# A hybrid attention block on one core: two weight loads taken out of line, earlier

## Chip, cores and metric

The kernel runs on 1 of the cores of a Trainium2 chip, as one program. The metric is the device time of one execution in microseconds (us); where several executions were timed, their median.

## What is computed

One decoder block over 512 tokens of width 2048, all float32: a norm of x, one wide projection, two groups of eight (A) and sixteen (B) heads, a gate, an out-projection with the residual, and a last norm.

```python
h = _rmsnorm(x, norm_g[l])
proj = h @ w_in[l]
(qa, kca, vca, ksa, vsa, kwa, vwa, za, ga, qb, kb, vb, zb) = jnp.split(proj, offsets, axis=-1)
...
y_a = o_a.reshape(B, S, WIDTH_A) * jax.nn.silu(za)    # compressed, selected and window attention, gated
qb = _rope(_heads(qb, N_HEADS_B, HEAD_DIM_B)).reshape(B, S, N_KV_B, GROUP_B, HEAD_DIM_B)
o_b = _banded_attention(qb, _rope(_heads(kb, N_KV_B, HEAD_DIM_B)), _heads(vb, N_KV_B, HEAD_DIM_B),
                        WIN_B, sink=sinks[l].reshape(N_KV_B, GROUP_B))
y_b = o_b.reshape(B, S, WIDTH_B) * jax.nn.silu(zb)
x = x + jnp.concatenate([y_a, y_b], axis=-1) @ w_out[l]
return _rmsnorm(x, final_g)
```

The second group is B. Its keys come from 128 columns of `w_in`, which the kernel calls `wkb` and loads as two units of 128 x 1024.

## The kernel before

**Split words.** TensorE (PE) multiplies in a reduced float32 format. Every operand is therefore split into a high word, made by a copy on ScalarE (ACT), and a low word, the rest, made by a subtraction on VectorE (DVE); a product is three matmuls (`mm3`, lines 119 to 121): high by high, high by low, low by high. A weight unit of 128 x 1024 is loaded by `load_unit` (L85): SyncE (SP) queues the DMA into a raw buffer (L88), ACT makes `whi` (L92), DVE makes `wlo` (L93).

**Buffers.** There are four raw buffers of one tile each, raw0 to raw3. `raw()` (L78) hands out raw0, raw1, raw2 in turn; raw3 lies in another pool and is used by the pairs of group A only, and later, in group B, by every second query tile `qs`. The split words have three buffers. A load into a raw buffer waits until its last reader is done, and a split waits until the matmuls on its word buffer are done.

**Group A.** For heads 1 to 7, `pair(h)` (L662) makes a head's query and gate projections together from four quarter units x1 to x4 of `wq`, each in one of the four raw buffers, by sums of the units (L672) and seven products on halves of x. For head 7 x1 lies in raw3, x2 in raw2, x4 in raw1 and x3 in raw0. The sums are x2+=x4, x4+=x1, x2+=x1 and x2+=x3, in this order; x1 is last read by x2+=x1, x4 by its split, x3 by x2+=x3 and x2 by the last split. `attn_a(h)` is the head's attention: scores `sp` (L546), exponentials `tt` on ACT (L562), scaling (L574), transposes `tp` (L584), the split words `ph` (ACT, L514) and `pl` (DVE, L515) of the transposed weights, and the products `op` (L590 to L607). While the pairs run, half of the even tiles of `xh` and `xl` hold other data.

**Between the groups.** `swap_x` (L626) loads the halves of `xh` and `xl` back from `xd`, as four DMAs (L630). Then `proj(wkb, parity=1)` (L882) starts group B: both wkb units are loaded first, the odd tiles of x are multiplied first, then the even ones. `proj(wz[16])` (L883) is the first query projection.

**Group B and the out-projection.** For i from 0 to 7: softmax of head pair i, the query projection of i + 1 from `wz[17 + i]`, the gate projection from `wz[24 + i]`, and `attn_b(i)`, which ends in two copies of `op` into `ob` on ACT (L877). Afterwards y is split (`yh`, L915) into memory that x held, and multiplied by the eight units of `wo0` (L1010).

**Order.** The program text is not the order of execution. A scheduler orders each engine's instructions by its own estimates, and each engine then runs its list in order, waiting on semaphores; so does SP with its DMAs. `tc.issue_after(a)` adds an instruction's wait for `a`. In group A and B, instructions of several heads and projections interleave on every engine.

Of the kernel before, what the change touches and what calls it, by code (L numbers as in the profile page):

```python
# [10 lines left out]
F32 = mybir.dt.float32  # L11
F32R = mybir.dt.float32r
AF = mybir.ActivationFunctionType
# [4 lines left out]
P = 128  # L18
# [10 lines left out]
MOVING, EVEN, STILL = 0, 16, 32  # L29
# [6 lines left out]
def hybrid_block(ctx, tc, xT, xtm, w0, w1s, w2s, wz, wq, wkb, wo0, wos, cw1, cw2, cpos, rope, tabs, sinks, gT, fg, out):  # L36
    nc = tc.nc
    pe, act, dve, pool = nc.tensor, nc.scalar, nc.vector, nc.gpsimd
# [32 lines left out]
    last = {}  # L71

    raws = [0]

    def weights(tag):
        return (wk if tag == "raw3" else wp).tile([P, 1024], F32, name="raw", tag=tag, bufs=1)

    def raw():  # L78
        raws[0] += 1
        return weights(f"raw{raws[0] % 3}")  # L80

    def words(place):
        return [wp.tile([P, 1088], F32R, name=nm, tag=nm)[:, place:place + 1024] for nm in ("whi", "wlo")]

    def load_unit(src, width, rawp=None, opening=False, place=EVEN):  # L85
        rw = rawp.tile([P, 1024], F32, name="raw", tag="raw") if rawp else raw()
        hi, lo = words(place)
        last["dma"] = (nc.scalar if opening else nc.sync).dma_start(rw[:, :width], src).ins  # L88
        if opening:
            dve.tensor_copy(hi[:, :width], rw[:, :width])  # L90
        else:
            last["hi"] = act.activation(hi[:, :width], rw[:, :width], AF.Copy).ins  # L92
        last["lo"] = dve.tensor_tensor(out=lo[:, :width], in0=rw[:, :width], in1=hi[:, :width].bitcast(F32),  # L93
                                       op=ALU.subtract).ins
        return hi, lo
# [77 lines left out]
    for k in range(KT):  # L173
        if k == 0:
            hi, lo = load_unit(w0[0, :, 0, 0:512], 512, opening=True)
            xr = load_x(k)
        else:
            xr = load_x(k)
            hi, lo = load_unit(w0[0, :, k // 2, (k % 2) * 512:(k % 2) * 512 + 512], 512)
# [88 lines left out]
    even = [x.rearrange("p (m e) s -> p e m s", e=2)[:, 0, :, 0:256].bitcast(F32) for x in (xh, xl)]  # L268
# [54 lines left out]
    for u in range(KT // 2):  # L323
        hi, lo = load_unit(w0[1, :, u], 1024)
# [58 lines left out]
    for g in range(2):  # L383
        act.activation(KH[g][:, 0:CMP], kct[:, g * 32:g * 32 + 32], AF.Copy)
        dve.tensor_tensor(out=KL[g][:, 0:CMP], in0=kct[:, g * 32:g * 32 + 32], in1=KH[g][:, 0:CMP].bitcast(F32),
                          op=ALU.subtract)
# [6 lines left out]
    for u in range(8):  # L393
# [6 lines left out]
            writes.pop(0)()  # L400
        if u in (2, 3, 5, 6):
            build()
    def proj(src, parity=None, jobs=None):
        ps = psp.tile([P, S], F32, name="pj", tag="pj")
        ready = []
        ks = list(range(KT))
        if parity is not None:
            ks = list(range(parity, KT, 2)) + list(range(1 - parity, KT, 2))
        for i, k in enumerate(ks):
            while len(ready) < (2 if jobs or parity is not None or k >= 8 else 1):  # L410
                ready.append(load_unit(src[:, len(ready)], 1024))
            if jobs and i in jobs:
                jobs[i]()
            hi, lo = ready[k // 8]
            js = slice((k % 8) * P, (k % 8) * P + P)
            mm3(ps, hi[:, js], lo[:, js], xh[:, k, :], xl[:, k, :], i == 0, i == KT - 1)
        return ps
# [42 lines left out]
    def z_evac(ps):  # L460
        zr = wk.tile([P, S], F32, name="zr", tag="t2", bufs=1)
        st = wk.tile([P, S], F32, name="st", tag="st")
        dve.tensor_tensor(out=zr, in0=ps, in1=rstdb, op=ALU.mult)
        act.activation(st, zr, AF.Tanh, scale=0.5)
        dve.scalar_tensor_tensor(out=st, in0=st, scalar=1.0, in1=zr, op0=ALU.add, op1=ALU.mult)
        return st

    def q_rope(ps, cos, sin, t1=None):
        if t1 is None:
            t1 = wk.tile([P, S], F32, name="t1", tag="t1", bufs=1)  # L470
        t2 = wk.tile([P, S], F32, name="t2", tag="t2", bufs=1)
        rope_mul(t1, t2, ps, cos, sin)
        pool.tensor_tensor(out=t1, in0=t1, in1=t2, op=ALU.add)
        return t1
# [151 lines left out]
    def swap_x(source):  # L626
        for part in range(2):
            ms = slice(4 * part, 4 * part + 4)
            for e in range(2):
                nc.sync.dma_start(even[e][:, ms], source[e, :, ms])  # L630

    def forms_back(f, ms):
        for e, (v, k) in enumerate(((VH, KH), (VL, KL))):
# [90 lines left out]
    for h in range(8):  # L724
        if h < FIRST:
            qq = q_evac(q0, cosA, sinA)
            st = z_evac(proj(wz[8], 0))
            lows, highs = slice(0, 4), slice(4, 8)
            first = []
            with tc.issue_after(last["dma"]):  # L730
                first.append(load_quarter(wq[0], tags[0], 3))
                forms_back(0, lows)
                forms_back(1, lows)
            for c, quarter in zip(tags[1:], (0, 2, 1)):
                with tc.issue_after(last["dma"]):
                    first.append(load_quarter(wq[0], c, quarter))
            with tc.issue_after(last["dma"]):
                for f in (2, 3):
                    forms_back(f, lows)
                    forms_back(f, highs)  # L740
        else:
            qq, st = pair(h, *first) if h == FIRST else pair(h)
        attn_a(h, *qq, st)
        if h == 3:
            for e in range(2):
                nc.sync.dma_start((KH, KL)[e][0].bitcast(F32), Kd[e])
            for e in range(2):
                nc.sync.dma_start((VH, VL)[e][:, 0].rearrange("p t w c -> p (t w c)").bitcast(F32), Vd[e])
# [10 lines left out]
    cosB, sinB = cosA, sinA  # L759
# [90 lines left out]
    def attn_b(i, tts, st):  # L850
        g = i // 4
        op = psob.tile([P, 2, S], F32, name="opb", tag="opb")
        for kt in (0, 2, 3, 1):
            tp = pst.tile([P, S], F32, name="tp", tag="tp")
            nsl = 2 if kt < 3 else 1
            for v in range(2):
                for s in range(nsl):
                    qt = kt + s
                    c0 = 0 if (s == 1 or qt == 0) else P
                    o = (v * nsl + s) * P  # L860
                    pe.transpose(tp[:, o:o + P], tts[qt][:, v, c0:c0 + P], ident)  # L861
            oc = op[:, :, kt * P:(kt + nsl) * P]
            if nsl == 2:
                ph, pl = split_pt(tp)
                for v in range(2):
                    es = slice(v * 256, v * 256 + 256)
                    pe.matmul(oc[:, v], VB[:, kt, g, :], ph[:, es], start=kt == 0, stop=False)
                    pe.matmul(oc[:, v], VB[:, kt, g, :], pl[:, es], start=False, stop=kt == 1)
            else:
                pd = wk.tile([P, 256], F32, name="pd", tag="pd", bufs=1)  # L870
                act.activation(pd, tp[:, 0:256], AF.Copy)
                for v in range(2):
                    pe.matmul(oc[0:64, v], vbf[:, kt, g * 64:g * 64 + 64], pd[:, v * P:v * P + P], start=False, stop=False)
        ob = wb.tile([P, S], F32, name="ob", tag="ob")
        for v in range(2):
            hs = slice(v * 64, v * 64 + 64)
            act.activation(ob[hs], op[64:128, v, :], AF.Copy)  # L877
            dve.tensor_tensor(out=ob[hs], in0=op[0:64, v, :], in1=ob[hs], op=ALU.add)
        finish(8 + i, ob, st)

    kb1 = wk.tile([P, S], F32, name="kb1", tag="xr", bufs=1)
    q_rope(proj(wkb, parity=1), cosB, sinB, kb1)  # L882
    q2 = qb_evac(proj(wz[16]), 0)  # L883
    build_k(kb1, 0)
    build_v()
    for i in range(8):
        tts = softmax_b(i, q2)
        if i < 7:
            q2 = qb_evac(proj(wz[17 + i]), i + 1)
        if i == 0:  # L890
            build_k(kb1, 1)
        st = z_evac(proj(wz[24 + i]))
        if i == 7:
            psb.close()
            xstack.close()
            so1 = ctx.enter_context(sb("so1", side="right"))
            yh = [so1.tile([P, S], F32R, name=f"yh{f}") for f in range(16)]
            yl = [so1.tile([P, S], F32R, name=f"yl{f}") for f in range(16)]
            psf1 = ctx.enter_context(tc.tile_pool(name="psf1", bufs=2, space=PSUM, side="right"))
        attn_b(i, tts, st)  # L900
        if i in (1, 2, 3, 4):
            y_back(i - 1)
# [105 lines left out]

    acc = banks(0)
    for u in range(8):  # L1010
        hi, lo = load_unit(wo0[:, u], 1024)
        for j in range(2):
            f = 2 * u + j
            ws = slice(j * 512, j * 512 + 512)
            for t in range(NQ):
                ts = slice(t * P, (t + 1) * P)
                mm3(acc[t], yh[f][:, ts], yl[f][:, ts], hi[:, ws], lo[:, ws], f == 0, f == 15)
        combos(u)
# [3 lines left out]
    for t in range(NQ):  # L1022
        v = xs0[t // 2][:, t % 2, :]
# [18 lines left out]
    for n in range(1, 4):  # L1042
        xs.append([late(2 * n - 2 + T) for T in range(2)])
        src = wos[n - 1]
# [287 lines left out]
```

## Time and profile before

| | us |
|---|---|
| median of 3 runs | 826.01 |
| the three runs | 823.29, 826.01, 827.65 |
| the profiled execution | 823.73 |
| its span, first to last instruction | 822.0 |
| outside the span | 1.73 |
| PE busy | 805.1 |
| DVE busy | 664.5 |
| ACT busy | 484.0 |

The profile is one execution; its times are us from the start of the span. "Busy" leaves out waiting, branching and issuing of DMAs. Matmuls are pipelined, so the duration of one is longer than its distance from the next, and the starts tell how fast PE goes. An idle time in brackets stands before the instruction, with what ended it. "SPq" is the queue in which SP issues DMAs; the time beside it is that of the issue, not of the transfer.

### The profile page before, as it was taken

How to read it: one execution, taken by the hardware profiler on the slowest of the kernel's cores; microseconds unless marked ns; L12 is line 12 of the kernel's file. 1: busy time of each engine (PE TensorE's matmuls, PEld its weight loads, DVE VectorE, ACT ScalarE, POOL GpSimd, SP SyncE). 2: the span in 40 equal slices, each digit the busy share in tenths (PEclk: the TensorE clock that was granted, in tenths of full speed). 3: DMA queues.
4: the chain of work that ended last, by engine and by line, in shares of the span. 5: the costliest groups of instructions: out<-in, count | busy, mean ns of one | idle time of the engine just before them, and what ended most of it. 6: DMA issues, size and time to landing. Idle time of an engine off the chain costs nothing.

```text
span 822.0 us, 14132 instructions
## 1 busy us (share of the span) xinstructions
PE 805.1 (98%) x5278; PEld 731.4 (89%) x5278; DVE 664.5 (81%) x1326; ACT 484.0 (59%) x1026; POOL 67.1 (8%) x54
## 2 busy tenths in 40 slices
PE   9999999999999999999999999999999999999996
PEld 7788898989999999999888888888888888999996
DVE  6869786967889899899766688887687798877895
ACT  6744456564767687786665365645444657543545
POOL 3600002020000000000011121011001000110000
PEclk9999999999999999999999999999999999999998
DMA  9665886899321332423633321222222227797845
GB/s 326 197 205 167 279 289 208 262 332 331 103 89 29 116 84 91 163 91 112 227 111 102 99 90 57 77 80 76 77 78 77 78 61 253 226 264 188 252 90 205
DMA packets 52116, 128.30 MB, mean 156 GB/s; under 512 B 4944, under 2 KB 17232, under 8 KB 52048
## 3 DMA queue, kind: packets, MB, share of 16 engines
q1 hardware_dynamic: 50032, 120.59, 44.4%
q0 software_dynamic: 1728, 6.29, 4.4%
q8 instruction: 41, 0.67, 0.3%
q10 hardware_dynamic: 288, 0.52, 0.2%
q14 instruction: 27, 0.22, 0.1%
HBM read 110.31 MB, written 17.07 MB: 155 GB/s over the span
## 4 chain that ended last, share of the span: by engine, by line
PE 78%; DVE 8%; DMA 7%; ACT 4%; issue 3%; SPq 0%; DVEq 0%; ACTq 0%; POOLq 0%
PE pj L121 14%; PE pj L120 14%; PE pj L119 14%; PE bank L121 4%; PE bank L119 4%; PE bank L120 4%; PE oa L120 3%; PE oa L121 3%; PE oa L119 3%; PE sp L546 3%; DMA rw<-wos 2%; PE tp L861 2%; DVE wlo L624 1%; PE tp L584 1%; DMA xr<-xT 1%
## 5 line engine op out<-in xcount | busy, mean ns | idle before, releaser
L121 PE MATMUL pj<-xh,wlo 128*128 128x512 f32 (+1 forms) x560 | 194.7, 348 | 1.8 <-DVE wlo L624 1.8
L119 PE MATMUL pj<-xh,whi 128*128 128x512 f32 (+1 forms) x560 | 195.0, 348 | 1.4 <-ACT whi L92 1.4
L120 PE MATMUL pj<-xl,whi 128*128 128x512 f32 (+1 forms) x560 | 194.6, 347 | 0.0
L93 DVE TENSOR_TENSOR wlo<-raw,whi 128x1024 fp32r<-128x1024 f32 (+2 forms) x102 | 115.4, 1134 | 35.2 <-ACT whi L92 34.3
L92 ACT ACTIVATE whi<-raw 128x1024 fp32r<-128x1024 f32 (+1 forms) x101 | 95.1, 944 | 75.1 <-PE pj L120 21.5
L121 PEld LDWEIGHTS pj<-xh,wlo 128*128 128x128 f32 x560 | 105.4, 188 | 15.3 <-DVE wlo L624 2.4
L119 PEld LDWEIGHTS pj<-xh,whi 128*128 128x128 f32 x560 | 105.3, 188 | 13.9 <-ACT whi L92 1.6
L120 PEld LDWEIGHTS pj<-xl,whi 128*128 128x128 f32 x560 | 105.3, 188 | 12.8 <-issue 0.7
L624 DVE TENSOR_TENSOR wlo<-raw,whi 128x1024 fp32r<-128x1024 f32 x49 | 59.5, 1221 | 9.3 <-ACT whi L623 9.2
L623 ACT ACTIVATE whi<-raw 128x1024 fp32r<-128x1024 f32 x49 | 51.1, 1054 | 21.7 <-PE pj L120 6.2
L120 PE MATMUL oa<-wlo,yh 128*128 128x256 f32 (+1 forms) x168 | 50.2, 299 | 0.4 <-DVE wlo L1160 0.4
L119 PE MATMUL oa<-whi,yh 128*128 128x256 f32 (+1 forms) x168 | 49.9, 298 | 0.6 <-ACT yh L915 0.6
L121 PE MATMUL oa<-whi,yl 128*128 128x256 f32 (+1 forms) x168 | 49.5, 298 | 0.0
L840 ACT ACTIVATE ttb<-ttb,sums 128x256 f32<-128x256 f32 (+1 forms) x64 | 30.1, 471 | 26.3 <-DVE sums L833 25.8
L514 ACT ACTIVATE ph<-tp 128x512 fp32r<-128x512 f32 x56 | 32.3, 592 | 22.3 <-PE tp L584 16.2
L515 DVE TENSOR_TENSOR pl<-tp,ph 128x512 fp32r<-128x512 f32 x56 | 38.0, 686 | 4.5 <-ACT ph L514 4.3
L120 PE MATMUL bank<-wlo,xh 128*128 128x256 f32 (+1 forms) x128 | 40.1, 316 | 0.1
L121 PE MATMUL bank<-whi,xl 128*128 128x256 f32 (+1 forms) x128 | 39.7, 312 | 0.0
L119 PE MATMUL bank<-xh,whi 128*128 128x512 f32 x96 | 36.8, 394 | 1.3 <-ACT whi L92 1.0
L119 PE MATMUL bank<-whi,xh 128*128 128x256 f32 (+1 forms) x128 | 36.5, 317 | 1.3 <-ACT whi L92 1.3
L120 PE MATMUL bank<-xl,whi 128*128 128x512 f32 x96 | 36.9, 390 | 0.0
L562 ACT ACTIVATE tt<-tt,sums 128x128 f32<-128x128 f32 (+3 forms) x64 | 35.3, 554 | 1.6 <-DVE sums L552 1.5
(356 smaller groups left out, 2169.3 us busy)
## 6 DMA issues: line engine op xcount, KB each, us to landing
raw<-wz SPq DMA_DIRECT2D x36, 512.0 KB, 3.9
raw<-wq SPq DMA_DIRECT2D x28, 512.0 KB, 4.0
raw<-cw SPq DMA_DIRECT2D x16, 512.0 KB, 5.1
raw<-wos SPq DMA_DIRECT2D x12, 512.0 KB, 5.4
rw<-wos SPq DMA_DIRECT2D x10, 512.0 KB, 4.8
xr<-xT SPq DMA_DIRECT2D x16, 256.0 KB, 4.8
raw<-w SPq DMA_DIRECT2D x8, 512.0 KB, 4.2
fd<-ft SPq DMA_DIRECT2D x4, 1024.0 KB, 6.0
```

What stands on the lines that cost most here:

```text
L92: last["hi"] = act.activation(hi[:, :width], rw[:, :width], AF.Copy).ins
L93: last["lo"] = dve.tensor_tensor(out=lo[:, :width], in0=rw[:, :width], in1=hi[:, :width].bitcast(F32), op=ALU.subtract).ins
L119: pe.matmul(ps, ah, bh, start=first, stop=False, skip_group_check=go_on)
L120: pe.matmul(ps, ah, bl, start=False, stop=False, skip_group_check=go_on)
L121: recent["mm"] = pe.matmul(ps, al, bh, start=False, stop=last, skip_group_check=go_on).ins
L514: act.activation(ph, tp, AF.Copy)
L515: dve.tensor_tensor(out=pl, in0=tp, in1=ph.bitcast(F32), op=ALU.subtract)
L546: pe.matmul(sp[:, a:b], qq[:, qs], kk[0][:, ko:ko + b - a], start=pi == 0, stop=pi == 2)
L562: act.activation(tv, tv, AF.Exp, bias=mn[:, i, 1 + w:2 + w], scale=-1.0, accum_out=dn[:, i, 1 + w:2 + w])
L623: act.activation(hi, src, AF.Copy)
L624: last["lo"] = dve.tensor_tensor(out=lo, in0=src, in1=hi.bitcast(F32), op=ALU.subtract).ins
L840: act.activation(tv, tv, AF.Exp, bias=mn[:, e, v:v + 1], scale=-1.0, accum_out=dn[:, e, v:v + 1])
```

## The change

Three things. While head 7's pair is written down, the two units of `wkb` get the buffers raw3 and raw1, and their DMAs are tied behind the pair's last load, the second behind the first. `swap_x`'s four DMAs are tied behind the last weight load, so behind both. `proj(wkb)` takes the loaded buffers; `raws[0] += 1` makes the rotation of raw0 to raw2 skip one place, so every later unit lies one buffer further than before (the first unit of `wz[16]` in raw1, where it lay in raw2). Second, the first unit of `wo0` is loaded and split after the gate projection of i = 6, ahead of that of i = 7, whose two units so come after it. Third, head pair 6's two copies into `ob` wait for that unit's ACT split. In the built order of each engine, lists are the same up to head 7, differ in places through the start of group B, and are nearly the same from there on.

```diff
-    def load_unit(src, width, rawp=None, opening=False, place=EVEN):
-        rw = rawp.tile([P, 1024], F32, name="raw", tag="raw") if rawp else raw()
+    def load_unit(src, width, rawp=None, opening=False, place=EVEN, loaded=None):
+        if loaded is None:
+            rw = rawp.tile([P, 1024], F32, name="raw", tag="raw") if rawp else raw()
+            last["dma"] = (nc.scalar if opening else nc.sync).dma_start(rw[:, :width], src).ins
+        else:
+            rw = loaded
         hi, lo = words(place)
-        last["dma"] = (nc.scalar if opening else nc.sync).dma_start(rw[:, :width], src).ins
...
-    def proj(src, parity=None, jobs=None):
+    def proj(src, parity=None, jobs=None, loaded=()):
...
-                ready.append(load_unit(src[:, len(ready)], 1024))
+                ready.append(load_unit(src[:, len(ready)], 1024,
+                                       loaded=loaded[len(ready)] if loaded else None))
...
     def swap_x(source):
...
-                nc.sync.dma_start(even[e][:, ms], source[e, :, ms])
+                with tc.issue_after(last["dma"]):
+                    nc.sync.dma_start(even[e][:, ms], source[e, :, ms])
...
             qq, st = pair(h, *first) if h == FIRST else pair(h)
+        if h == 7:
+            early = []
+            for u in range(2):
+                early.append(weights(("raw3", "raw1")[u]))
+                with tc.issue_after(last["dma"]):
+                    last["dma"] = nc.sync.dma_start(early[u], wkb[:, u]).ins
         attn_a(h, *qq, st)
...
-            act.activation(ob[hs], op[64:128, v, :], AF.Copy)
+            with ExitStack() as behind:
+                if i == 6:
+                    behind.enter_context(tc.issue_after(last["hi"]))
+                act.activation(ob[hs], op[64:128, v, :], AF.Copy)
...
-    q_rope(proj(wkb, parity=1), cosB, sinB, kb1)
+    raws[0] += 1
+    q_rope(proj(wkb, parity=1, loaded=early), cosB, sinB, kb1)
...
         st = z_evac(proj(wz[24 + i]))
+        if i == 6:
+            first_out = load_unit(wo0[:, 0], 1024)
...
-        hi, lo = load_unit(wo0[:, u], 1024)
+        hi, lo = load_unit(wo0[:, u], 1024) if u else first_out
```

## Prediction

> **What bounds the kernel now.** I read the page first, then the PE's waits, then windows of 60 us, and only then the stretch in which the change works. The page's engine rows and its chain:
>
> ```profile
> span 822.0 us, 14132 instructions
> ...
> PE 805.1 (98%) x5278; PEld 731.4 (89%) x5278; DVE 664.5 (81%) x1326; ACT 484.0 (59%) x1026; POOL 67.1 (8%) x54
> ...
> PE 78%; DVE 8%; DMA 7%; ACT 4%; issue 3%; SPq 0%; DVEq 0%; ACTq 0%; POOLq 0%
> ```
>
> TensorE (PE) is busy for 805.1 of 822.0 us: all that any reordering can win is in the 17 us left, and most of those are in the opening and the end. Where the change works, the windows (us; busy time of PE, PEld, DVE, ACT, POOL; granted clock; DMA share; GB/s) say:
>
> ```profile
> 400.00:405.00 5.00, 3.09 (x22) 2.46 (x22) 2.26 (x5) 2.66 (x6) 0.00 (x0) 1.00 1.05 376
> ...
> 420.00:480.00 60.00, 60.00 (x320) 51.45 (x319) 37.79 (x77) 31.14 (x65) 10.64 (x6) 1.00 0.32 103
> 480.00:540.00 60.00, 60.00 (x331) 51.28 (x330) 51.72 (x156) 36.05 (x102) 4.50 (x2) 1.00 0.22 71
> ```
>
> One hole of 1.91 us at 400 to 405, with the DMA engines full (share 1.05), and then no idle PE at all. The page "Perfetto Trace Analysis" of the Trainium skill, section Identifying the Most-Contended Engine, would judge PE's headroom by the weight loads' busy share, not by the matmuls'. By that rule 89% on the page leaves 11%, some 90 us. The rows differ: where PE waits for nothing (420 to 540) PEld stands at 51.4 of 60, so about 86% is full here, and I take nothing from that headroom.
>
> **The hole that the first edit is to close.** The PE timeline (start, duration, operation, idle before it and what ended that), and the chain of waits over the same stretch:
>
> ```profile
> 401.61 0.28 PE L120 MATMUL pj<-pu,whi 128*128 128x256 f32 x1
> 401.73 0.28 PE L121 MATMUL pj<-pu,wlo 128*128 128x256 f32 x1
> 403.45 0.50 PE L119 MATMUL pj<-xh,whi 128*128 128x512 f32 x1 [1.45 <-ACT whi L92]
> 403.79 0.40 PE L120 MATMUL pj<-xl,whi 128*128 128x512 f32 x1
> 404.64 0.39 PE L590 MATMUL op<-ph,VH 128*128 128x256 f32 x1 [0.46 <-ACT ph L514]
> 404.86 0.39 PE L121 MATMUL pj<-xh,wlo 128*128 128x512 f32 x1
> 405.09 0.39 PE L119 MATMUL pj<-xh,whi 128*128 128x512 f32 x1
> ```
> ```profile
> 395.44 6.82 DMA raw<-wkb
> ```
>
> Matmuls overlap, so I cost a stall by starts: a 256-column one takes 0.12 us (401.61 to 401.73), a 512-column one 0.23 (404.86 to 405.09). From 401.73 to 403.45 is 1.72, so 1.60 lost; from 403.79 to 404.64 is 0.85, so 0.62 lost. Together **2.22 us**. Both come from one transfer, the wkb unit that is issued at 395.44 and lands at 402.26. ScalarE (ACT) shows how one late load makes two stalls:
>
> ```profile
> 396.04 1.06 ACT L623 ACTIVATE whi<-raw 128x1024 fp32r<-128x1024 f32 x1
> ...
> 402.34 1.06 ACT L92 ACTIVATE whi<-raw 128x1024 fp32r<-128x1024 f32 x1 [2.41 <-DMA raw<-wkb]
> 403.30 0.71 ACT L562 ACTIVATE tt<-tt,sums 128x512 f32<-128x512 f32 x1
> ...
> 404.01 0.57 ACT L514 ACTIVATE ph<-tp 128x512 fp32r<-128x512 f32 x1
> ```
>
> ACT stands at L92 for 2.41 us, and behind it wait an exponential (L562) and the copy ph (L514) for which PE waits next. The DMA queue of SyncE (SP) tells why the load is late:
>
> ```profile
> 387.99 0.33 SPq L88 DMA_DIRECT2D raw<-wkb  x1
> 394.43 0.37 SPq L630 DMA_DIRECT2D xl<-xd  x1
> 394.89 0.46 SPq L630 DMA_DIRECT2D xh<-xd  x1
> 395.44 0.45 SPq L88 DMA_DIRECT2D raw<-wkb  x1
> ...
> 398.38 0.34 SPq L88 DMA_DIRECT2D raw<-wz  x1
> 400.95 0.33 SPq L496 DMA_DIRECT2D yd<-st  x1
> ...
> 407.53 0.39 SPq L501 DMA_DIRECT2D yp<-yd  x1
> ```
>
> By the built order the load at 387.99 is the second wkb unit (buffer raw1). The first takes raw0, which the last sum of pair(7) frees, and stands behind two loads of x's halves.
>
> **Edit 1, part by part.** Removed: the place at 395.44. Added: nothing; the same two transfers and splits. Moved: the first unit goes to raw3, whose last reader is the sum x2+=x1, and the second stays in raw1 but is queued second:
>
> ```profile
> 389.07 1.22 DVE L672 TENSOR_TENSOR raw<-raw 128x1024 f32<-128x1024 f32 x1
> ```
>
> That ends at 390.29, so both are queued by 390.8, ahead of x's halves. A load of this size takes
>
> ```profile
> L88 SPq DMA_DIRECT2D raw<-wkb x2: 333/394/454, 388.0 to 395.4; - x2
> ...
> DMA to landing us min/median/max: 3.6/5.2/6.8
> ```
>
> 3.6 us (the one issued at 388, alone) to 6.8 (among the halves): the first lands between 393.9 and 397.1, and I take 394, the row without company. Even 397.1 does: in the built order the split L92 now stands right after L623, whose row ends at 397.10. It then ends at 398.2, PE asks for it at 401.85, and its DVE half (1.13 us, a row below) has until two matmuls later. ACT had been free since 399.93 (402.34 less 2.41), so the exponential (0.71) and ph (0.57) then end at 401.2, while PE's new order has twelve 512-column matmuls (2.7 us) ahead of ph's product: needed at 404.6. Both stalls go: minus 2.22 us, and 0 at the other end if something else takes their place.
>
> Moved past on SP: x's halves start 0 to 1 us later, for the tail of the second wkb load. In place of the late wkb unit a wz unit (the z projection's, into raw0) is now queued among them, so they land about when they do now. PE's order has pair(7)'s last product and half of wkb's own matmuls ahead of them, and no wait of PE's in this trace names them. Cost 0; without that cover 1 us. The first unit of wz[16], issued now at 398.38 into raw2, goes into raw1 instead, behind the second wkb split and behind yp<-yd: about 408. It is the one thing that becomes late, and the rival below prices it. Later units come three buffers ahead as before; between 420 and 540 PE waits for nothing, and the rest of the schedule, being PE-bound, moves up whole.
>
> **Edit 2.** The out-projection's first unit is loaded before the last z projection's two units and split in the place of ACT that held the first of these; these move one place each. ACT's three places (timeline), and the one PE stall near them:
>
> ```profile
> 623.11 1.06 ACT L92 ACTIVATE whi<-raw 128x1024 fp32r<-128x1024 f32 x1
> 629.22 1.04 ACT L92 ACTIVATE whi<-raw 128x1024 fp32r<-128x1024 f32 x1
> 634.06 1.06 ACT L92 ACTIVATE whi<-raw 128x1024 fp32r<-128x1024 f32 x1 [3.80 <-issue]
> ```
> ```profile
> 649.97 0.60 ACT L877 ACTIVATE ob<-opb 64x512 f32<-64x512 f32 x1 [2.65 <-PE opb L868]
> 650.67 1.06 ACT L92 ACTIVATE whi<-raw 128x1024 fp32r<-128x1024 f32 x1
> 651.63 1.66 ACT L915 ACTIVATE yh<-yp 128x512 fp32r<-128x512 f32 x3
> ```
> ```profile
> 635.86 0.40 PE L119 MATMUL pj<-xh,whi 128*128 128x512 f32 x1
> ...
> 652.30 0.50 PE L119 MATMUL oa<-whi,yh 128*128 128x512 f32 x1 [0.55 <-ACT yh L915]
> ```
>
> The last z projection starts on PE at 635.86; its words would come from the place of 629.22, three us ahead even with the DVE half. The added wait (head 6's output copy ob waits for that split) is met 25 us early, so nothing queues behind it. The stall of 0.55 us at 652.30 stays: yh stands behind a split (650.67, the third out unit's) that the built order keeps there. So 0, between 0.55 won and 1.06 (one split, if ob or yh were pushed by one) lost.
>
> **The sum.** 822.0 minus 2.2 gives a span of 819.8; with the 1.73 us that the profiled execution's 823.73 has outside its span, 821.5. That execution is 2.28 under the median of the runs shown (826.01, from 823.29 to 827.65), so the median I forecast is 826.01 - 2.2 = **823.8**. About 0.5% (4.1 us) is what a measurement here can tell from no change, and the forecast, at 0.27%, is inside it.
>
> **Rivals.** *More than forecast.* The lost time hangs on one transfer's landing while the DMA engines are full, so it may be longer in the median run than in the profiled one, which was among the fastest. If the whole 2.28 us between them is this wait, it goes too: 821.5. For it: landings from 3.6 to 6.8. Against: the opening's loads can vary as well, and they stay. *Given back.* The next late thing costs the same 2.2: 826.0. For it: a schedule moved up by 2 us meets every later transfer earlier. Against: the empty waits from 420 on. *Slower.* The unit of wz[16] now waits on SP for yp, which waits for yd to land, and its split on ACT holds the next ph:
>
> ```profile
> L88 SPq DMA_DIRECT2D raw<-wz x3: 328/332/345, 398.4 to 408.9; - x3
> ...
> DMA to landing us min/median/max: 4.8/5.1/8.0
> ```
>
> Queued at about 408.2, it lands at 413.0 to 416.2. PE reaches the first product of that ph after 43 matmuls of 0.23, 31 of 0.12 and some 1.7 us of small ones from 401.85, at about 417, and the one with pl at 417.8. From landing to pl lie the split's ACT half (1.06), its DVE half and two steps of pl's size, by the page's groups (busy, mean ns of one):
>
> ```profile
> L93 DVE TENSOR_TENSOR wlo<-raw,whi 128x1024 fp32r<-128x1024 f32 (+2 forms) x102 | 115.4, 1134 | 35.2 <-ACT whi L92 34.3
> ...
> L515 DVE TENSOR_TENSOR pl<-tp,ph 128x512 fp32r<-128x512 f32 x56 | 38.0, 686 | 4.5 <-ACT ph L514 4.3
> ```
>
> 1.06 + 1.13 + 2 x 0.69 = 3.6 us, so up to a landing of 414.2 nothing is lost. At 5.1 us it holds by 0.9; at 8.0 it loses 2.0 and the gain is nearly gone; if yp too comes 8.0 us after yd, not the 6.6 of now (400.95 to 407.53), it loses 3.4 and the kernel is 1.2 slower: 827.2. It ends slower from a landing 8.2 us after the issue. What holds ph there is ACT's order, seen above at 402.34. The Trainium skill's "TensorE: Matmul & The Clock Gate", section Architectural detail, calls ScalarE's queue strict FIFO, which speaks against putting any split ahead of its data; the 2.41 us row agrees.
>
> **How the numbers follow.** Forecast 0.55 (823.8), more than forecast 0.20 (821.5), given back 0.15 (826.0), slower 0.10 (827.2). Medians of three may scatter by 1.3 us (an estimate from the spread of the runs shown), so faster by over 0.5% (below 821.9) gets 0.20, slower by over 0.5% (above 830.1) 0.05, within 0.75. The range takes 821.5 and 826.0 with some scatter: 820.8 to 827.2.
>
> **What would show it.** Right: both wkb loads issued before 391; no idle PE at L119 between 400 and 405; ACT's L92 after L623 without a DMA wait; 652's stall of 0.5 still there; the start of the out-projection some 2.2 us earlier. Wrong: a wait of ACT's whi for raw<-wz near 409 to 414 longer than 5 us with idle PE at 417; idle PE that x's halves end; or the same 2 us reappearing behind 540.

## The result and the profile after

| | before | after |
|---|---|---|
| median, us | 824.68 (20 runs, 822.29 to 828.91) | 822.23 (20 runs, 819.47 to 825.33) |
| ratio, 95% interval | | 0.996 (0.9946 to 0.9975) |
| profiled span, us | 822.0 | 818.9 |

The changed kernel is 2.45 us faster beside the kernel before, against a forecast of 2.2. One repeat gave 0.9987 (0.9966 to 1.0009). The executions of one kernel scatter by 6 to 8 us, so a better figure is the mean over all that were timed in this study: 825.02 us for the kernel before (114 executions), 822.70 for the changed one (32): **2.3 us, give or take 0.75**. Each of the two measurements by itself gives less certain figures, by the means 2.5 us here and 1.1 in the repeat.

Line numbers move by 3 to 17: L119 to L121 are L122 to L124 now, L92 is L95, L514 is L518, L590 is L594, L623 is L627, L915 is L932; the early wkb loads are issued at L753. The page's engine rows after:

```profile
span 818.9 us, 14128 instructions
...
PE 805.4 (98%) x5278; PEld 733.0 (90%) x5278; DVE 665.5 (81%) x1326; ACT 483.6 (59%) x1026; POOL 66.8 (8%) x54
```

PE works as long as before and idles 3.4 us less (span less busy time: 13.5 against 16.9). The windows of the same stretches (us; busy PE, PEld, DVE, ACT, POOL; clock; DMA share; GB/s) say where:

```profile
400.00:405.00 5.00, 5.00 (x34) 4.51 (x33) 4.44 (x9) 2.61 (x6) 0.00 (x0) 1.00 1.03 366
420.00:480.00 60.00, 60.00 (x311) 51.07 (x310) 42.27 (x84) 31.90 (x71) 13.40 (x7) 1.00 0.31 102
480.00:540.00 60.00, 60.00 (x327) 51.12 (x326) 51.63 (x157) 34.12 (x93) 4.54 (x2) 1.00 0.24 75
```

The hole at 400 to 405 is gone, with the DMA engines as full as before (share 1.03 against 1.05): the same bytes move, in another order. SP's queue and ACT over that stretch:

```profile
388.76 0.81 SPq L753 DMA_DIRECT2D raw<-wkb  x2
392.83 0.38 SPq L635 DMA_DIRECT2D xl<-xd  x1
...
407.43 0.32 SPq L505 DMA_DIRECT2D yp<-yd  x1
407.84 0.38 SPq L88 DMA_DIRECT2D raw<-wz  x1
408.31 0.38 SPq L771 DMA_DIRECT2D cosA<-rope  x1
```
```profile
394.44 1.06 ACT L627 ACTIVATE whi<-raw 128x1024 fp32r<-128x1024 f32 x1
395.39 1.05 ACT L95 ACTIVATE whi<-raw 128x1024 fp32r<-128x1024 f32 x1
...
399.08 0.60 ACT L518 ACTIVATE ph<-tp 128x512 fp32r<-128x512 f32 x1
400.33 1.06 ACT L95 ACTIVATE whi<-raw 128x1024 fp32r<-128x1024 f32 x1
...
411.83 1.06 ACT L95 ACTIVATE whi<-raw 128x1024 fp32r<-128x1024 f32 x1 [4.69 <-PE pj L124]
```

Both wkb loads go out by 389.6, ahead of every half of x. The first split runs at 395.39 with no wait in front, where in the kernel before ACT waited 2.41 us for it; ph is done by 399.7. The 4.69 us in front of the last row are ACT's wait for wz[16]'s first unit. PE is named as the one that ended it, but the unit itself landed only at 411.7 (3.9 us after its issue), and in experiment 1 the same wait (4.30 us) is put down to the transfer. On PE wkb's twelve products follow the last product of the pair without a gap, and ph's product comes behind them:

```profile
400.13 0.28 PE L124 MATMUL pj<-pu,wlo 128*128 128x256 f32 x1
400.25 0.40 PE L122 MATMUL pj<-xh,whi 128*128 128x512 f32 x1
...
402.77 0.39 PE L124 MATMUL pj<-xh,wlo 128*128 128x512 f32 x1
402.99 0.28 PE L594 MATMUL op<-ph,VH 128*128 128x256 f32 x1
...
648.33 0.50 PE L122 MATMUL oa<-whi,yh 128*128 128x512 f32 x1 [0.55 <-ACT yh L932]
```

The last product of the pair starts 1.60 us earlier than in the trace before (400.13 against 401.73): that is chance, from stretches that the change leaves alone (in the thirteen traces of this study it starts between 399.8 and 402.2, early and late ones among the kernels with edit 1). The out-projection starts 3.97 us earlier (648.33 against 652.30). So the change brought **2.37 us** in between. This stretch, from the pair's last product to the out-projection, repeats far better than the whole time: 250.57 and 250.64 us in the two traces without edit 1 (the kernel before and experiment 2), 248.10 to 248.20 in the seven with edit 1 in which nothing else makes PE wait there or takes a wait out (the changed kernel, experiments 1, 4, 7 and 9, and the first kernel of experiment 8). From the start of the out-projection to the end the changed kernel took 170.6 us and the kernel before 169.7, which gave 0.9 back; in all traces that last stretch takes 169.5 to 175.0 us, and the pace, described at the end, explains most of that.

### The profile page after: what moved, and what is told of

The parts are those of the page before. It is cut to its first block, busy times and chain, and to the rows that moved or that the text cites. A ratio compares the mean times of both kernels' runs of the same rounds, so it can differ in the third digit from the quotient of the medians.

```text
span 818.9 us, 14128 instructions
## 1 busy us (share of the span) xinstructions
PE 805.4 (98%) x5278; PEld 733.0 (90%) x5278; DVE 665.5 (81%) x1326; ACT 483.6 (59%) x1026; POOL 66.8 (8%) x54
## 4 chain that ended last, share of the span: by engine, by line
PE 85%; DVE 6%; DMA 5%; ACT 3%; issue 1%; POOL 0%; ACTq 0%; POOLq 0%; DVEq 0%
PE pj L124 15%; PE pj L123 15%; PE pj L122 15%; PE bank L122 5%; PE bank L123 5%; PE bank L124 5%; PE sp L550 3%; PE oa L123 3%; PE oa L124 3%; PE oa L122 2%; PE tp L588 2%; DMA rw<-wos 2%; PE tp L872 2%; DMA ch<-wos 1%; DVE wlo L937 1%
## 5 line engine op out<-in xcount | busy, mean ns | idle before, releaser
L124 PE MATMUL pj<-xh,wlo 128*128 128x512 f32 (+1 forms) x560 | 194.9, 348 | 1.8 <-DVE wlo L628 1.8
L122 PE MATMUL pj<-xh,whi 128*128 128x512 f32 (+1 forms) x560 | 194.6, 348 | 0.0
L95 ACT ACTIVATE whi<-raw 128x1024 fp32r<-128x1024 f32 (+1 forms) x101 | 94.9, 943 | 78.5 <-PE pj L123 22.8
L124 PEld LDWEIGHTS pj<-xh,wlo 128*128 128x128 f32 x560 | 105.4, 188 | 15.0 <-DVE wlo L628 2.4
L122 PEld LDWEIGHTS pj<-xh,whi 128*128 128x128 f32 x560 | 105.3, 188 | 12.1
L627 ACT ACTIVATE whi<-raw 128x1024 fp32r<-128x1024 f32 x49 | 51.2, 1055 | 22.3 <-PE pj L123 7.2
L122 PE MATMUL oa<-whi,yh 128*128 128x256 f32 (+1 forms) x168 | 50.0, 298 | 0.6 <-ACT yh L932 0.6
L124 PE MATMUL oa<-whi,yl 128*128 128x256 f32 (+1 forms) x168 | 49.5, 298 | 0.0
L518 ACT ACTIVATE ph<-tp 128x512 fp32r<-128x512 f32 x56 | 32.3, 591 | 14.6 <-PE tp L588 8.4
L124 PE MATMUL bank<-whi,xl 128*128 128x256 f32 (+1 forms) x128 | 39.7, 312 | 0.0
L122 PE MATMUL bank<-whi,xh 128*128 128x256 f32 (+1 forms) x128 | 36.4, 316 | 1.3 <-ACT whi L95 1.3
L122 PE MATMUL bank<-xh,whi 128*128 128x512 f32 x96 | 37.4, 401 | 0.0
```

Of the source, the lines that this page charges most:

```text
L122: pe.matmul(ps, ah, bh, start=first, stop=False, skip_group_check=go_on)
L124: recent["mm"] = pe.matmul(ps, al, bh, start=False, stop=last, skip_group_check=go_on).ins
L518: act.activation(ph, tp, AF.Copy)
L627: act.activation(hi, src, AF.Copy)
```

## The experiments

**1. Edit 1 alone** (`e1_edit1`).

```diff
-            with ExitStack() as behind:
-                if i == 6:
-                    behind.enter_context(tc.issue_after(last["hi"]))
-                act.activation(ob[hs], op[64:128, v, :], AF.Copy)
+            act.activation(ob[hs], op[64:128, v, :], AF.Copy)
...
-        if i == 6:
-            first_out = load_unit(wo0[:, 0], 1024)
...
-        hi, lo = load_unit(wo0[:, u], 1024) if u else first_out
+        hi, lo = load_unit(wo0[:, u], 1024)
```

> Edit 1 alone: the two first key units (wkb) are loaded into the third and first buffer ahead of x's four halves; the first out-projection unit is loaded and split where the kernel before does it. Theory (the whole gain is the hole at 400 to 405 us that closes, 2.2 us; edit 2 is worth nothing): 2.0 to 2.6 us faster than before, ratio 0.9968 to 0.9976, no idle PE ahead of wkb's products, and the stall of some 0.5 us at 645 to 655 is still there. Rival (edit 2 carries part of the gain of 2.45 us, or costs something that edit 1 pays for): 1.5 us or less, or 3 us or more, with a row at 640 to 670 us in which the two traces differ by it.

Measured: 822.55 us, ratio 0.9961 (0.9941 to 0.998). Its window of 400 to 405, and that of 640 to 660, which the changed kernel's trace shows with the same 19.45 us of PE:

```profile
400.00:405.00 5.00, 5.00 (x34) 4.51 (x33) 4.46 (x9) 2.61 (x6) 0.00 (x0) 1.00 1.02 359
...
640.00:660.00 20.00, 19.45 (x92) 15.68 (x91) 17.17 (x39) 15.95 (x33) 0.00 (x0) 1.00 0.18 53
```

From the pair's last product to the out-projection this trace takes 248.20 us, as the changed kernel's. Edit 1 brings the whole gain, and the wait of 0.55 us for yh stands without edit 2 as with it.

**2. Edit 2 alone** (`e2_edit2`): the lines that experiment 1 takes out, put into the kernel before.

> Edit 2 alone on the kernel before: the first out-projection unit is loaded and split ahead of the last head's output; wkb's units are loaded as before, the first of them behind x's halves. Theory (edit 2 is worth nothing): the ratio's interval holds 1.000, between 0.9994 and 1.0006; the hole at 400 to 405 us is still there with 1.9 to 2.3 us of lost PE time, and the stall at 645 to 655 keeps its 0.5 us. Rival (edit 2 is worth part of the gain): ratio 0.9994 or less, and the stall at 645 to 655 is shorter. Rival on the size (the wait for the first wkb unit varies between executions): the landing of that unit is more than 0.5 us away from 6.8 us after its issue, and the hole changes by the same.

Measured: 824.93 us, ratio 0.9997 (0.9975 to 1.0019). The PE timeline and ACT:

```profile
402.81 0.50 PE L119 MATMUL pj<-xh,whi 128*128 128x512 f32 x1 [1.52 <-ACT whi L92]
403.15 0.39 PE L120 MATMUL pj<-xl,whi 128*128 128x512 f32 x1
404.00 0.38 PE L590 MATMUL op<-ph,VH 128*128 128x256 f32 x1 [0.46 <-ACT ph L514]
```
```profile
401.70 1.06 ACT L92 ACTIVATE whi<-raw 128x1024 fp32r<-128x1024 f32 x1 [2.48 <-DMA raw<-wkb]
```

The interval alone would allow edit 2 up to 2 us either way, but the trace shows the hole whole (1.52 and 0.46 us idle, 1.45 and 0.46 before), and the wait at 651 is 0.55 as before. The trace also shows the hole in the kernel's old order a second time: this profiled execution took 826.89 us, 3.2 more than the 823.73 of the first, with the same hole. So the wait for wkb is not what made this execution slower, which speaks against the rival *more than forecast*.

**3. The same buffers, the other order** (`e3_halves_first`): the wkb loads behind x's halves.

```diff
-                with tc.issue_after(last["dma"]):
-                    nc.sync.dma_start(even[e][:, ms], source[e, :, ms])
+                last["xd"] = nc.sync.dma_start(even[e][:, ms], source[e, :, ms]).ins
...
+        with tc.issue_after(last["xd"]):
+            last["xd"] = last["dma"] = nc.sync.dma_start(early[u], wkb[:, u]).ins
```

> The changed kernel, with only the order of SP's queue turned round: the two wkb loads go into the third and first buffer as in the changed kernel, but behind x's four halves instead of ahead of them. Theory (the place in the queue matters, since the halves take the DMA engines' share): the first wkb unit is issued at about 391 to 396 us, lands 5 to 7 us later, ACT waits for it again, and the hole of 1 to 2.2 us comes back: ratio 0.998 to 1.000 against the kernel before. Rival (the buffer alone matters, since in the kernel before the first unit waits for a buffer that is freed late): the loads are issued as early as their buffers allow, land before 399.5 us, and the gain stays, ratio 0.9965 to 0.9975.

Measured: 824.62 us, ratio 0.9995 (0.9972 to 1.0017). SP's queue, ACT and PE:

```profile
395.61 2.28 SPq L758 DMA_DIRECT2D raw<-wkb  x2
```
```profile
406.30 1.06 ACT L95 ACTIVATE whi<-raw 128x1024 fp32r<-128x1024 f32 x1 [3.44 <-DMA raw<-wkb]
```
```profile
400.75 0.38 PE L122 MATMUL pj<-VH,whi 128*128 128x256 f32 x1 [0.40 <-DVE t L676]
...
407.41 0.50 PE L122 MATMUL pj<-xh,whi 128*128 128x512 f32 x1 [1.54 <-ACT whi L95]
...
408.67 0.50 PE L124 MATMUL pj<-xh,wlo 128*128 128x512 f32 x1 [0.52 <-DVE wlo L96]
```

The buffer is free by 389, when the changed kernel loads it, and that does not help: behind the halves the first load lands some 10.7 us after its issue, and PE waits again for its words, 1.54 and 0.52 us, although the scheduler, which saw the load late, had put over 5 us of other products ahead of wkb's. (The 0.40 us at 400.75 are a wait that this new order brings.) From the pair's last product to the out-projection it is 251.35 us, no better than the kernel before. The early place in the queue is what pays; the other buffers only make it possible.

**4. Other buffers, the same order** (`e4_raw1_raw0`).

```diff
-                early.append(weights(("raw3", "raw1")[u]))
+                early.append(weights(("raw1", "raw0")[u]))
...
-    raws[0] += 1
+    raws[0] += 2
```

> The changed kernel with other buffers for the two wkb units: the first buffer and the one that is freed last, instead of the third and the first; x's halves stay behind both loads, and the first unit of the next z projection (wz[16]) keeps the buffer that it had in the kernel before. Theory (the first unit's landing before 399.5 us is all that counts, the second has about 1.2 us of product time behind it, and the halves are needed only much later): the first unit lands by 392 us, the second is issued at about 395.5 us and lands by 400 us since no half is in its way, no idle PE at 400 to 405: ratio 0.9965 to 0.9976, as the changed kernel. Rival (the halves, now issued from 396 us on, land late enough to be waited for, or the second unit is late): a hole of 0.5 to 2 us at 402 to 412 us, ratio 0.998 to 0.9995.

Measured: 822.78 us, ratio 0.9974 (0.9953 to 0.9994). SP holds the second load until its buffer is free, and PE never waits:

```profile
387.85 7.44 SPq L753 DMA_DIRECT2D raw<-wkb  x2
395.35 0.43 SPq L635 DMA_DIRECT2D xh<-xd  x1
```
```profile
400.00:405.00 5.00, 5.00 (x34) 4.51 (x33) 4.36 (x10) 2.71 (x6) 0.00 (x0) 1.00 1.02 324
```

One unit that lands early is enough. x's halves are issued at 395.35, where the changed kernel issues them at 392.83; this trace runs 1.5 us behind that one (its pair ends with a product at 401.59, against 400.13), so they are 1.1 us later, and still not waited for. The prediction's 1 us for them without their cover was never touched.

**5. The wait that edit 2 leaves** (`e5_y_first`): head 0's output words ahead of the third out unit's split.

```diff
...
+            if f == 0:
+                units = [first_out, load_unit(wo0[:, 1], 1024)]
+                with tc.issue_after(last["yh"]), tc.issue_after(last["yl"]):
+                    units.append(load_unit(wo0[:, 2], 1024))
...
```

> The changed kernel, in which the first head's output words for the out-projection (yh, yl of head 0) go ahead of the third out-projection unit's split on ACT and on DVE. In all six traces so far PE waits 0.55 us there for ACT's yh, with or without edit 2, since ACT splits that unit first (1.06 us). Theory: the wait of 0.55 us at 645 to 655 us is gone or under 0.1 us, and the time falls by 0.5 us more than the changed kernel's, to a ratio of 0.995 to 0.997. Rival (the third unit's words, now 0.6 us later, or the buffers that yh lies in are late next): the same 0.3 to 0.6 us are lost within 10 us behind it, and the time is the changed kernel's.

Measured: 821.8 us over 8 runs, ratio 0.9962 (0.9945 to 0.9978): the changed kernel's time. The wait for yh is gone from the list of PE's waits, but the stage's next boundary has a new one; the PE timeline there:

```profile
696.14 0.38 PE L122 MATMUL oa<-whi,yh 128*128 128x256 f32 x1 [1.14 <-ACT whi L936]
696.73 0.38 PE L123 MATMUL oa<-wlo,ph 128*128 128x256 f32 x1 [0.21 <-DVE wlo L937]
```

The rival held, but some 47 us behind the old wait, not within 10: ACT runs without a break from 685 to 695, and the scheduler's new order on PE asks there for a second unit that ACT has not split yet. 0.55 us of waiting were exchanged for 1.15 more (1.35 here, 0.2 in the changed kernel).

**6. The rival on the slower side, made to happen** (`e6_late_z`): six useless copies beside wz[16]'s first unit.

```diff
+    for k in range(6):
+        pool.dma_start(dram(f"junk{k}", P, S), yd[5])
     q2 = qb_evac(proj(wz[16]), 0)
```

> The changed kernel with six copies of 0.25 MB each within device memory, of no use to the result, on GpSimd's queue from about 407.5 us on, at the time at which the changed kernel loads the first unit of the z projection behind wkb (issued at 407.8, landed at 411.7). They share the DMA engines with it and make it land later. Theory, from the prediction's rival on the slower side: ACT waits for it with the head's output words behind it; up to a landing of some 414 us nothing is lost, and from there PE loses as much as it lands later; with a landing of 416 to 420 us, 2 to 6 us lost, ratio 0.999 to 1.004. Rival (more slack than was reckoned, since PE has other products at hand): a landing of over 415 us with less than 0.5 us of idle PE at 414 to 425 us and a ratio under 0.998. If the copies delay the unit by less than 2 us, nothing is told.

Measured: 824.32 us, ratio 0.9988 (0.9973 to 1.0003). By the means, 824.36 against 822.70, 1.7 us of the gain are lost; in this trace, from the pair's last product to the out-projection (251.11 against 248.20), 2.9. This trace runs 2.0 us behind the changed kernel's (its second wkb split starts at 402.34 against 400.33). ACT, DVE and PE:

```profile
414.99 1.06 ACT L95 ACTIVATE whi<-raw 128x1024 fp32r<-128x1024 f32 x1 [5.84 <-DMA raw<-wz]
...
416.47 1.06 ACT L518 ACTIVATE ph<-tp 128x512 fp32r<-128x512 f32 x2
```
```profile
417.77 0.69 DVE L773 TENSOR_TENSOR cosA<-cosA,rstdb 128x512 f32<-128x512 f32 x1 [5.58 <-DMA cosA<-rope]
418.38 1.22 DVE L96 TENSOR_TENSOR wlo<-raw,whi 128x1024 fp32r<-128x1024 f32 x1
```
```profile
420.85 0.38 PE L595 MATMUL op<-pl,VH 128*128 128x256 f32 x1 [1.74 <-DVE pl L519]
...
432.39 0.33 PE L588 MATMUL tp<-ident,tt 128*128 128x128 f32 x1 [0.77 <-ACT tt L578]
```

The unit landed at 415.0, in the changed kernel's clock 413.0. (The expectation's 414 was not taken over to that clock, where the prediction's limit of 414.2 is 412.6.) The scheduler had pulled three more products, 0.7 us, ahead of the first one with pl, so by the prediction's sum nothing should be lost; PE lost 1.74 us, and 0.77 more behind it at 432. The reason is a step that the sum lacks: on DVE, cosA's product stands ahead of wlo, st and pl, and cosA landed 2.8 us after the unit. The same steps in the changed kernel's own trace (DVE, then PE):

```profile
412.53 0.69 DVE L773 TENSOR_TENSOR cosA<-cosA,rstdb 128x512 f32<-128x512 f32 x1 [2.16 <-DMA cosA<-rope]
413.14 1.22 DVE L96 TENSOR_TENSOR wlo<-raw,whi 128x1024 fp32r<-128x1024 f32 x1
...
414.88 1.28 DVE L519 TENSOR_TENSOR pl<-tp,ph 128x512 fp32r<-128x512 f32 x2
```
```profile
416.26 0.28 PE L595 MATMUL op<-pl,VH 128*128 128x256 f32 x1
```

The first pl is done at 414.88 + 0.69 = 415.57, 0.7 us before PE takes it. In experiment 6 cosA was 417.77 - 2.0 - 412.53 = 3.2 us later; 0.7 of slack and the 0.7 of products pulled ahead leave some 1.8, near the 1.74 seen.

**7. cosA and the unit ahead of yp** (`e10_cos_first`, with the copies; `e11_cos_alone`, without).

```diff
...
+    with tc.issue_after(last["cos"]):
+        last["z"] = last["dma"] = nc.sync.dma_start(first_z, wz[16][:, 0]).ins
...
+                if i == 3:
+                    behind.enter_context(tc.issue_after(last["cos"]))
+                    behind.enter_context(tc.issue_after(last["z"]))
                 y_back(i - 1)
```

> The kernel with the six copies that have no use, in which the load of cosA and that of the first z unit behind wkb go ahead of yp<-yd in SP's queue; both needn't wait for yd's landing, as yp does. In that kernel's trace PE waited 1.74 us for pl, and on DVE cosA's product stood in front of it, which waited 5.6 us for cosA's landing at 417.7, while the z unit had landed at 414.9. Theory (cosA is what was late, on DVE, and not the z unit on ACT): cosA lands ahead of the copies, PE's wait for pl at 415 to 421 us is under 0.5 us, ratio 0.996 to 0.998. Rival (the copies slow whatever is needed there, or the z unit is late next): a wait of over 1 us stays at 412 to 425 us, ratio 0.998 to 1.0.

> The changed kernel with the loads of cosA and of the first z unit behind wkb ahead of yp<-yd, and no copies. In the changed kernel's trace pl is done some 0.7 us before PE takes it, so nothing waits there. Theory: the slack grows to over 2 us, and the time is the changed kernel's: ratio 0.995 to 0.9975. Rival (in some executions of the changed kernel the 0.7 us do not suffice, which its median carries): 0.5 us or more faster than the changed kernel beside it; or yp, now later, is waited for at 520 us or later: slower by that.

Measured: with the copies 821.93 us, ratio 0.9979 (0.9962 to 0.9996); without them 823.15, ratio 0.9981 (0.996 to 1.0001); the changed kernel beside them 823.46 (experiment 9). The window of 412 to 425, of experiment 6 and then of this kernel with the copies:

```profile
412.00:425.00 13.00, 11.26 (x65) 9.51 (x64) 5.97 (x14) 5.96 (x13) 0.68 (x2) 1.00 0.60 206
```
```profile
412.00:425.00 13.00, 13.00 (x73) 11.29 (x73) 10.94 (x25) 7.63 (x18) 2.94 (x3) 1.00 0.74 263
```

The idle time is gone. Both loads moved here, so this run alone does not part cosA from the unit; the DVE rows of experiment 6 do. Without the copies the slack between pl and PE grew from 0.7 to 2.6 us and the time is not told from the changed kernel's (823.15 against 823.46, which would hide a difference of 1.6 us). In the traces nothing had used that slack up: in none of the eight with the early loads ahead of x's halves and without the copies does PE wait between 405 us and the out-projection.

**8. The pace of the last stage** (`e7_words_first`, and with experiment 5's edit `e8_both_first`): the second output stage's first two weight units split ahead of operand words that are needed later.

```diff
...
+            if m >= 6 and nm != "p":
+                after_first.append((nm, m, src))
+            else:
+                split_to(hi, lo, src)
...
         u3 = [halves(load(raw(), 0, g)) for g in range(2)]
+        if n == 1:
+            with tc.issue_after(last["hi"]), tc.issue_after(last["lo"]):
+                for nm, m, part in after_first:
+                    split_to(*ops[nm, m], part)
...
```

> The changed kernel, in which the first two weight units of the second output stage are split ahead of the last operand words, which are needed later. It is about something seen beside the change: from 700 us to the end the 256-column products follow each other at 113.3 ns in four of six traces and at 117.8 ns in two (532 or 512 of them in 720 to 780 us), the same clock throughout, and the pace changes only where PE has waited; the first such place is a wait of 0.2 us for wlo at 695 to 699 us, in front of which the pace is the fast one in all six. The slow pace costs 3 to 4 us in an execution, more than the change gains. Theory (a wait of PE sets the pace anew, without one it stays): no wait at 690 to 700 us, 113.3 ns from there to the next wait of PE, 0.4 us less lost at 695; fewer executions at the slow end, median ratio 0.993 to 0.996, if the wait at 712 us does not set it anew. Rival (the pace has another cause): the wait is gone, but the pace is slow from 695 us on with no wait in front, or the spread of the executions (5 to 8 us) and the median stay the changed kernel's.

> The two edits of the last kernels but one together on the changed kernel: the first head's output words ahead of the third out-projection unit's split, and the second output stage's first two units ahead of the last operand words. Theory: both waits (0.55 us at 648, 0.2 us with its restart of 0.15 us at 695) are gone, 0.9 us in all, and the pace of the last stage is the fast one up to the next wait: ratio 0.992 to 0.995. Rival: the waits are gone and the time comes back at the next wait of PE (700 to 715 us), ratio 0.995 to 0.997.

Measured: 824.07 us, ratio 0.9987 (0.9976 to 0.9997), and 823.52, ratio 0.9983 (0.9968 to 0.9998). By the means, 824.13 and 823.44, the first is 1.4 us slower than the changed kernel's 822.70, and the second is not told from it. The theory fell: the wait at 695 is gone (the first row below; 9.79 of 10.00 busy in the changed kernel), and the products follow at 117.8 ns from the first one on, with no wait in front. Starts in the first kernel's PE timeline:

```profile
690.00:700.00 10.00, 10.00 (x64) 9.03 (x63) 7.55 (x13) 6.42 (x14) 1.93 (x2) 1.00 0.93 233
```
```profile
695.56 0.28 PE L122 MATMUL oa<-whi,ph 128*128 128x256 f32 x1
695.67 0.28 PE L123 MATMUL oa<-wlo,ph 128*128 128x256 f32 x1
...
696.97 0.28 PE L122 MATMUL oa<-whi,ph 128*128 128x256 f32 x1
```

Twelve starts in 1.41 us. Besides, the moved words put new waits of 1.2 us in total at 721 to 725.

**9. The changed kernel once more** (`e9_after_again`).

> The changed kernel once more, beside the next two, for a second trace of it. Theory: ratio 0.995 to 0.9975; no idle PE at 400 to 405 us, ACT's first wkb split without a wait, the 0.55 us wait for yh at 645 to 655 us; the last stage at 113.3 or 117.8 ns a product after each wait, whatever the change did. What is lost beside that stage within 1 us of the first trace. Rival on the wait at 712 us (it belongs to the change, since it stood in all three kernels with the early wkb loads that reached it at the fast pace and in none of the two without them): it is there again if the stage starts at the fast pace; if it is not, it comes and goes with the transfers.

Measured: 823.46 us, ratio 0.9987 (0.9966 to 1.0009). In the trace the hole is closed and yh's wait is 0.55 us, as in the first; the out-projection starts at 648.22, 0.1 us from the first. But it took 174.1 us from the start of the out-projection to the end, where the first took 170.6. The window of 720 to 780 of the first trace, and of this one:

```profile
720.00:780.00 60.00, 60.00 (x532) 60.00 (x531) 48.10 (x58) 30.25 (x42) 5.22 (x6) 1.00 0.85 240
```
```profile
720.00:780.00 60.00, 60.00 (x512) 60.00 (x511) 47.29 (x55) 28.41 (x40) 5.22 (x6) 1.00 0.83 234
```

The same kernel, the same full clock (1.00), PE busy all the time, and 20 matmuls fewer in 60 us. The wait at 712 us was there again (0.34 us), now at the other pace, and missing in experiments 5 and 7 without copies, which have edit 1 too: it comes and goes with the transfers, and whether the change makes it likelier stays open.

## Why the prediction was right

**The hole.** Its steps held one by one. On the prediction's clock, which this trace runs 1.6 us ahead of, both loads go out between 390.4 and 391.2 (said: before 391), ACT's split has no wait, ph is done at 401.3 (said: 401.2); PE does not idle, and the out-projection starts 2.37 us earlier beyond that offset (said: some 2.2). Experiment 3 shows that the place in the queue did it, experiment 1 that edit 1 did all of it. Pooled by edit, the executions with edit 1 in its plain forms (changed kernel, experiments 1 and 4; 56) average 822.72 us, those without (before, experiment 2; 126) 825.02: 2.3 us. The forecast median, 823.8, lies 1.6 us above the measured 822.23 all the same, for it was reckoned from the median of three executions, 826.01, and that of twenty is 824.68: the difference was right, its base 1.3 us too high.

**A term that was small by 0.2.** The prediction took 2.22 us from the two stalls by their starts and left out that the first product after a wait is slow too: 403.45 to 403.79 is 0.34 us for a product of 0.23, and 404.64 to 404.86 is 0.22 for one of 0.12. With these 0.2 the hole was worth 2.4, and 2.37 to 2.5 is what the traces show.

**Edit 2.** Worth 0, as said, and its stall stayed, as said. Its range, 0.55 won to 1.06 lost, was not needed.

**More than forecast.** The 2.28 us between the profiled execution and the median are most likely not this wait: experiment 2's execution was 3.2 us longer with the same hole, and it lost its time from the start of the out-projection to the end (173.4 us against 169.7), by the pace of the last stage, which the prediction did not see. The other two executions behind that median have no trace, so for them this is not shown.

**Slower.** It did not come, and its sum was sound where it looked: it put PE's first product with ph at 417 and with pl at 417.8, and in this trace, 1.6 us early, they start at 415.44 and 416.26. The unit's wait on ACT was 4.69 us, under the 5 that it named as the sign. That the unit came in time was in part luck: on the prediction's clock it was issued at 409.4, not 408.2, since yp's load followed yd's by 7.6 us and not by 6.6, but it landed 3.9 us after its issue and not 5.1, and the two errors cancel. What was wrong is the step "from landing to pl": three steps on DVE and none for cosA's product, which stands ahead of them and waits for a transfer that is queued behind the unit. The real slack was 0.7 us, where the sum, in this trace's clock, left 0.8 to 0.9 for the unit's landing (412.6 against 411.7, and 411.8 for its split): nearly the same number from the wrong transfer, and experiment 6 shows that it is cosA's landing that decides.

## What to carry to other kernels

An engine's list runs in order, so a load is costed by the whole list that stands behind its first reader: here one late unit stopped PE twice, through the split itself and through the copy behind it. When a transfer is moved, look at everything that is queued behind it and at every wait that its readers' engines already have ahead of them; the slack of the moved kernel was set by the table cosA behind the unit, not by the unit. And before a gain of 0.3% is hunted or doubted, compare two traces of one kernel stretch by stretch: what differs there is no part of the change.

## What the runs showed of the hardware

**One size of product, two paces.** In the last stage every matmul has 256 columns and new weights. In all traces its starts lie 113.3 or 117.8 ns apart (a mean over nine or more in a row), at the same granted clock, and over that stage the difference is 3 to 4 us, more than the change brings. The pace seldom changes except where PE has waited; after a wait it settles within eight products. Where PE entered the stage through its short wait (0.2 us, or 1.1 in experiment 5), it took the quicker pace in nine traces of eleven; where it entered without one (the two kernels of experiment 8), the other in both. Most of the later waits left it as it was. In experiment 1 a wait of 0.5 us at 712 turned it from the quicker to the other, in the second kernel of experiment 8 a smaller disturbance at 711 did the reverse. The weight loads are busy all through this stage (PEld 60.00 of 60.00), and in the mean they take 188 ns at the quicker pace and, by group, 188 to 192 at the other. The Trainium skill's "TensorE: Matmul & The Clock Gate", section Back-to-back issue gap, says that the distance of matmuls is set by both the load and the product, pipelined through a reorder window. It gives one distance for a size; the runs show two. That a wait lets the loads get ahead of the products is a guess: no trace here shows which load was taken when, so what sets the pace stays open.

**A wait costs more than its idle time.** After a wait of PE for another engine a first product with 512 columns took 0.33 to 0.34 us to the next start instead of 0.23, and one with 256 columns 0.22 to 0.23 instead of 0.11 to 0.12, wherever the next product followed without a wait of its own.
